# Six small constants placed first in SBUF, so that the 8 KB, 4 KB and 2 KB buffers begin at multiples of 1 KB

## The chip, the core and the metric

One core of a Trainium2 chip. Its engines are TensorE (PE in the profile; its weight loads are listed apart as PEld), VectorE (DVE), ScalarE (ACT), GpSimd (POOL) and SyncE (SP, which here only issues DMAs). Operands lie in SBUF, 128 partitions with an address within the partition; matmul results go to PSUM. The metric is the device time of one launch in microseconds, as the median of several runs.

## The reference

Two transformer blocks over one sequence of 512 tokens with 1024 features, all in float32. Cut to its shape:

```python
# first block
h = rms_norm(x, norm_g);  proj = h @ w_in
o_diff = diff_attention(...)                 # 4 heads, two softmaxes each
o_nsa  = g0 * compressed + g1 * selected + g2 * window     # 8 heads, 2 key heads
x = x + concat([o_diff * silu(dz), o_nsa * silu(nz)]) @ w_out
# second block
h = rms_norm(x, g_mix);  proj = h @ w_in_2
mixed = sigmoid gates over (short conv @ w_branch_a) and (top-256 attention @ w_branch_b)
x = x + mixed @ w_out_2
h = rms_norm(x, g_ffn)
x = x + (silu(h @ w_ffn_gate) * (h @ w_ffn_up)) @ w_ffn_down      # 1024 -> 2816 -> 1024
out = rms_norm(x, g_final)
```

## The kernel before

**Every large product is three matmuls.** A float32 operand is split into a rounded part (hi, written by ScalarE, lines 206 and 1272) and a remainder (lo, a subtraction on VectorE or GpSimd, lines 208 and 1273). `mm3` (line 171 on) then issues hi·hi, hi·lo and lo·hi into one PSUM bank, each a matmul of line 164 with its own load of the stationary operand: the load of the next matmul runs beside the matmul before it.

**Which operand stands still and which streams.** `gen_ii` (activations stand still, 256 to 320 weight columns stream), `gen_tt` (activations stand still, 512 weight columns stream), `gen_i` (weights stand still, 512 activation columns stream), and in the feed-forward `Pair.product` (line 1330): weights stand still, 256 columns of `hA` stream, 24 matmuls in a row. Between two products the feed-forward runs 12 matmuls of the down projection (`dn`, a `gen_ii`: activations `act` stand still, 256 weight columns stream).

**Where buffers lie.** A buffer belongs to a class (a tag of the pool), and a class is laid out when it is first asked for, in the order of the program text. Ahead of all classes lie 4,096 bytes of scratch and four constants of the framework, 32 bytes each, so the first class begins at 4,224, that is 128 past a multiple of 1,024. Before, the order was: `kf` (3 buffers of 4 KB), `k4` (13 of 4 KB), `k2` (19 of 2 KB), then `mhalf` (32 bytes), `identF` (512), the small class `sm` (28 of 96), `identR` (512), `ones` (32), then `k8` (13 of 8 KB), then the rest. So:

| class | what lies in it | start before | past a multiple of 1 KB |
|---|---|---|---|
| kf, k4 | raw weights, their hi and lo parts (`raw`, `whi`, `wlo`, `wh`, `wl`), attention probabilities `PTa` | 4,224 | 128 |
| k2 | 2 KB work tiles, weights of the down projection, `PTb` | 69,760 | 128 |
| k8 | activations as matmul operands: `hT`, `hA`, `act`, `qk`, `dV`, `yc`, `at`, `mg`, `oTd`, `oTn` | 112,448 | 832 |

Within a class every buffer has the same remainder, since their sizes are multiples of 1 KB. The parts of a buffer that matmuls read start a multiple of 512 bytes further on, except in the products with 264, 280 and 320 streamed columns. A pair of streamed and stationary operand from two different classes (k8 with k4 or k2) therefore starts 192 or 704 bytes apart, counted within 1 KB; a pair from one class, or from k4 and k2, starts 0 or 512 apart. The weights of the first two products of pairs 0 and 2 of the feed-forward (`begin`, line 1294, with `early`) are the one case in which the split weights are put into `k8` buffers: there the same product of 24 matmuls runs with both operands in `k8`.

Of the kernel before, what the change touches and what calls it, by code (L numbers as in the profile page):

```python
# [15 lines left out]
P = 128  # L16
# [31 lines left out]
class Kernel:  # L48
# [26 lines left out]
    def t(self, cls, shape, dt=F32, name="w"):  # L75
        return self.pool.tile(shape, dt, name=name, tag=cls, bufs=BUFS[cls])
# [104 lines left out]
    def tick(self):  # L181
        c, self.cost = getattr(self, "cost", 0.0), 0.0
        if self.filling and not self.busy:
            self.credit -= c
        self.spend(c)
# [66 lines left out]
def build(tc, pool, psum, dram, h):  # L252
    nc = tc.nc
    K = Kernel(tc, pool, psum, dram, h)
# [16 lines left out]
    S, MAKE = Lazy(), {}  # L271
# [10 lines left out]
    def f32(ap):  # L282
        return ap.bitcast(F32)
# [108 lines left out]
    def new_hT():  # L392
        return [[t("k8", [P, 4, T], F32R, "hT") for _ in range(2)] for _ in range(2)]
# [26 lines left out]
        return f  # L420


    xin = [t("kf" if tt < 3 else "k4", [P, D], F32, "xt") for tt in range(NT)]
    gB1 = t("k4", [P, D], F32, "gB")

    def x_load(tt):
        for c in range(XP):
            a = slice(c * D // XP, (c + 1) * D // XP)
            S["x"] = tc.keep_in_program_order(nc.sync.dma_start(xin[tt][:, a], x[tt * P:(tt + 1) * P, a])).ins

    grow = t("k2", [P, P], F32, "grow")[0:8]
    nc.scalar.dma_start(grow, h["norm_g"][0].rearrange("(r c) -> r c", c=P))
    x_load(0)

    mhalf = K.const([P, 1], "mhalf")
    V.memset(mhalf, -0.5)
    identF = K.const([P, P], "identF")
    make_identity(nc, identF)
    warm = ps([P, P], name="warm")
    for _ in range(WARM[0]):  # L440
# [13 lines left out]
        K.tr(warm, identF, identF)  # L454
    identR = K.const([P, P], "identR", F32R)
    G.tensor_copy(identR, identF)
    ones = K.const([P, 1], "ones")
    V.memset(ones, 1.0)


    S["hT"] = new_hT()

    NV = 65
    maskc = K.const([P, T], "maskc")
    DM = K.const([P, T], "DM")
    cmask = K.const([P, 4, 32], "cmask")
    rowok = K.const([P, 1], "rowok")
    qsc = K.const([P, 4, 2, 4], "qsc")
    cw2 = K.const([P, 2, 2, 64], "cw2")
    rbT = K.const([8, 32], "rbT")  # L470
# [2 lines left out]
    vec = K.const([P, NV], "vec")  # L473
    GD = K.const([P, 64], "GD")
    GN = K.const([P, 3, 64], "GN")
    c01 = K.const([P, 2], "c01")

    def constants():
        vrow = t("k2", [P, P], F32, "vrow")
# [336 lines left out]
        return evac  # L816


    KC = K.const([P, 64], "KC")

    def cmp_evac(m, o):
        v = m % 2
# [68 lines left out]
    def cmp_finish():  # L891
        for v in range(2):
# [5 lines left out]
            if v == 0:  # L898
# [12 lines left out]
                def go(kd=kd):  # L911
                    pk = ps([P, 64], name="pt")
                    K.tr(pk, kd[0:64].rearrange("p a d -> p (a d)"), identF[0:64, 0:64])
                    A.copy(KC, pk)
                    tick()
# [18 lines left out]
    def cmp_attention(g):  # L934
        st = {}

        def rows(tt):
            sc = ps([P, 4, 32], name="sc")
            for c in range(4):
                K.mm(sc[:, c, :], f32(S["nQ%d" % g][:, c, tt * P:(tt + 1) * P]), KC[:, g * 32:(g + 1) * 32],  # L940
                     c == 0, c == 3)
# [682 lines left out]
def emit(tc, h, stage="all"):  # L1624
    with tc.tile_pool(name="sb", bufs=1) as pool, \
            tc.tile_pool(name="ps", bufs=1, space=bass.MemoryType.PSUM) as psum, \
            tc.tile_pool(name="dr", bufs=1, space=bass.MemoryType.DRAM) as dram, \
            contextlib.nullcontext():
        build(tc, pool, psum, dram, h)
# [18 lines left out]
```

## Time and profile before

| | us |
|---|---|
| median of 3 runs | 1069.44 (1069.07 to 1070.16) |
| the profiled execution, its own time | 1070.19 |
| its span, first to last instruction | 1068.4 |
| TensorE busy in the span | 1043.4 (98%) |
| VectorE busy | 720.0 (67%) |
| ScalarE busy | 556.2 (52%) |
| GpSimd busy | 396.8 (37%) |
| DMA engines, queue 1, share of 16 | 32.6% |

The clock granted to TensorE is 0.994 over the whole span. Busy time of a matmul is modelled and overlaps with the next, so the rate of matmuls is read from starts, not from durations: the timeline merges equal neighbours into one row with its start and its count. In a triple hi·hi, hi·lo, lo·hi the first two have one name and the third another, so the starts of every second row are three matmuls apart.

### The profile page before, as it was taken

What the parts mean: (1) busy time and instruction counts of PE and PEld (TensorE: products, weight loads), DVE (VectorE), ACT (ScalarE), POOL (GpSimd) and SP (SyncE); (2) the same over time, 40 slices, a digit from 0 to 9 for tenths busy, and PEclk for the clock granted to TensorE, in tenths of its full rate; (3) what the DMA queues carried; (4) which work ended last, traced back from release to release, by engine and by line L of the source; (5) the groups of instructions that cost most, each with busy time, mean ns of one, the idle gap of its engine ahead of it and who ended that gap; (6) DMA issues with size and microseconds to landing.
All of it is one profiled execution on the core that took longest, in us unless ns stands there. A gap on an engine that the chain in (4) does not pass through costs nothing.

```text
span 1068.4 us, 18973 instructions
## 1 busy us (share of the span) xinstructions
PE 1043.4 (98%) x7257; PEld 962.7 (90%) x7257; DVE 720.0 (67%) x1468; ACT 556.2 (52%) x1155; POOL 396.8 (37%) x403
## 2 busy tenths in 40 slices
PE   6999999999999999999999999999999999999997
PEld 6999898899779899888888888989999999999995
DVE  5787467446994646999423653979987777777724
ACT  5476678647884445632323776436544444444433
POOL 3442357466367322112115875920012112121241
PEclk8999999999999999999999999999999999999999
DMA  5344421221114435335322323641433323333122
GB/s 167 114 138 136 102 62 41 58 82 60 57 43 129 140 92 167 100 98 155 112 79 69 90 70 108 237 139 60 158 109 119 117 82 100 94 114 109 31 90 79
DMA packets 128085, 109.69 MB, mean 103 GB/s; under 512 B 20393, under 2 KB 119154, under 8 KB 127994
## 3 DMA queue, kind: packets, MB, share of 16 engines
q1 hardware_dynamic: 126906, 105.83, 32.6%
q0 software_dynamic: 1072, 2.65, 0.7%
q8 instruction: 57, 0.93, 0.4%
q14 instruction: 34, 0.28, 0.1%
q10 hardware_dynamic: 16, 0.00, 0.0%
HBM read 103.13 MB, written 6.84 MB: 103 GB/s over the span
## 4 chain that ended last, share of the span: by engine, by line
PE 90%; DVE 4%; POOL 2%; ACT 2%; issue 1%; DMA 0%; SPq 0%; POOLq 0%; DVEq 0%; ACTq 0%
PE acc L164 76%; PE pt L178 5%; PE sc L164 4%; PE o L164 4%; POOL wlo L208 1%; ACT p L636 1%; DVE p L634 1%; DVE acc L1513 0%; POOL mg L1213 0%; DVE mg L1216 0%; PE warm L178 0%; DMA gv<-in_diff_k_norm_g 0%; ACT junk L380 0%; DVE PTa L653 0%; ACT whi L206 0%
## 5 line engine op out<-in xcount | busy, mean ns | idle before, releaser
L208 POOL TENSOR_TENSOR wlo<-raw,whi 128x1024 fp32r<-128x1024 f32 (+4 forms) x99 | 205.0, 2075 | 444.4 <-ACT whi L206 365.5
L164 PE MATMUL acc<-hA,wh 128*128 128x256 f32 x1264 | 218.0, 279 | 0.7 <-ACT wh L1272 0.7
L206 ACT CAST whi<-raw 128x1024 fp32r<-128x1024 f32 (+4 forms) x143 | 132.0, 924 | 125.1 <-PE acc L164 80.1
L164 PE MATMUL acc<-hT,whi 128*128 128x512 f32 x608 | 194.5, 398 | 0.0
L164 PEld LDWEIGHTS acc<-hA,wh 128*128 128x128 f32 x1264 | 189.0, 189 | 1.3 <-ACT wh L1272 0.9
L164 PE MATMUL acc<-whi,hT 128*128 128x256 f32 (+3 forms) x896 | 180.7, 290 | 1.0 <-DVE hT L402 1.0
L164 PE MATMUL acc<-hA,wl 128*128 128x256 f32 x584 | 162.4, 278 | 0.0
L164 PEld LDWEIGHTS acc<-whi,hT 128*128 128x128 f32 x896 | 144.1, 189 | 1.7 <-DVE hT L402 1.2
L164 PEld LDWEIGHTS acc<-hT,whi 128*128 128x128 f32 x608 | 112.2, 188 | 24.5 <-ACT r L1512 0.2
L164 PE MATMUL acc<-whi,act 128*128 128x256 f32 (+1 forms) x640 | 130.0, 289 | 0.0
L164 PE MATMUL acc<-wlo,hT 128*128 128x256 f32 (+3 forms) x448 | 128.6, 288 | 0.0
L164 PE MATMUL acc<-hT,wlo 128*128 128x512 f32 x304 | 120.9, 398 | 0.0
L164 PEld LDWEIGHTS acc<-hA,wl 128*128 128x128 f32 x584 | 109.6, 188 | 0.0
L164 PEld LDWEIGHTS acc<-whi,act 128*128 128x128 f32 x640 | 103.9, 188 | 2.5
L164 PE MATMUL acc<-wlo,act 128*128 128x256 f32 (+1 forms) x320 | 92.3, 289 | 0.0
L636 ACT ACTIVATE p<-p,s 128x128 f32<-128x128 f32 (+3 forms) x128 | 72.2, 565 | 29.9 <-DVE s L634 27.1
L164 PEld LDWEIGHTS acc<-wlo,hT 128*128 128x128 f32 x448 | 84.4, 189 | 0.4
L1272 ACT CAST wh<-raw 128x1024 fp32r<-128x1024 f32 x55 | 57.6, 1052 | 50.1 <-PE acc L164 43.6
L1273 DVE TENSOR_TENSOR wl<-raw,wh 128x1024 fp32r<-128x1024 f32 x51 | 63.3, 1245 | 29.8 <-PE acc L164 17.3
L208 DVE TENSOR_TENSOR wlo<-raw,whi 128x1024 fp32r<-128x1024 f32 (+5 forms) x44 | 53.6, 1221 | 42.3 <-ACT whi L206 42.2
L164 PEld LDWEIGHTS acc<-hT,wlo 128*128 128x128 f32 x304 | 57.2, 188 | 13.1
L164 PEld LDWEIGHTS acc<-wlo,act 128*128 128x128 f32 x320 | 60.1, 188 | 1.3
(279 smaller groups left out, 2044.4 us busy)
## 6 DMA issues: line engine op xcount, KB each, us to landing
raw<-in_w_in SPq DMA_DIRECT2D x52, 512.0 KB, 3.6
raw<-in_w_ffn_gate SPq DMA_DIRECT2D x28, 512.0 KB, 3.6
raw<-in_w_ffn_up SPq DMA_DIRECT2D x22, 512.0 KB, 4.6
raw<-in_w_ffn_down SPq DMA_DIRECT2D x36, 256.0 KB, 5.2
raw<-in_w_out SPq DMA_DIRECT2D x16, 512.0 KB, 3.3
raw<-in_cmp_w SPq DMA_DIRECT2D x8, 512.0 KB, 3.6
raw<-in_w_in SPq DMA_DIRECT2D x10, 384.0 KB, 3.4
rel_all<-rel_rows POOLq DMA_DIRECT2D x1, 2560.0 KB, 18.0
```

The lines of the kernel that those rows point to most:

```text
L164: self.nc.tensor.matmul(out, lhsT, rhs, start=start, stop=stop, skip_group_check=True)
L178: self.nc.tensor.transpose(out, in_, ident)
L206: self.nc.scalar.copy(hi, raw)
L208: (self.nc.gpsimd if every and self.split and self.split % every == 0 else self.nc.vector).tensor_tensor(lo, raw, hi.bitcast(F32), op=OP.s ...
L634: V.tensor_tensor_reduce(out=p[:, :n], in0=sc[:, :n], in1=bias, scale=-scale, scalar=3e38, op0=OP.add, op1=OP.min, accum_out=nm)
L636: S["exp"] = A.activation(p[:, :n], p[:, :n], AF.Exp, scale=-1.0, bias=nm, accum_out=z).ins
L1272: A.copy(hi, src)
L1273: eng.tensor_tensor(lo, src, f32(hi), op=OP.subtract)
```

## The change

Six constants that were asked for at different places are asked for first: `identF` (512 bytes), `KC` (256), `mhalf`, `ones`, `rowok` and `c01` (32 each), together 896 bytes. 4,224 + 896 = 5,120, a multiple of 1,024. And the first `k8` buffer is asked for right after the first `k2` buffer, ahead of `sm` and `identR`. In the built program all three big classes now start at a multiple of 1 KB (kf 5,120, k2 70,656, k8 109,568), and every pair of matmul operands from them starts 0 or 512 bytes apart within 1 KB, in the products with 264, 280 and 320 columns 0 or 256 or other multiples of 32.

Nothing else differs. On each of the five engines the instructions stand in the same order, with the same shapes, the same waits and the same semaphore values; only addresses, buffer numbers in names and line numbers differ. The order in the program text moved only where buffers are named: no instruction is added, removed or moved.

```diff
+    identF, KC = K.const([P, P], "identF"), K.const([P, 64], "KC")
+    mhalf, ones, rowok = [K.const([P, 1], name) for name in ("mhalf", "ones", "rowok")]
+    c01 = K.const([P, 2], "c01")
     xin = [t("kf" if tt < 3 else "k4", [P, D], F32, "xt") for tt in range(NT)]
     gB1 = t("k4", [P, D], F32, "gB")
...
     x_load(0)
-
-    mhalf = K.const([P, 1], "mhalf")
+    S["hT"] = new_hT()
+
     V.memset(mhalf, -0.5)
-    identF = K.const([P, P], "identF")
     make_identity(nc, identF)
...
-    ones = K.const([P, 1], "ones")
     V.memset(ones, 1.0)
-
-
-    S["hT"] = new_hT()
...
-    rowok = K.const([P, 1], "rowok")
...
-    c01 = K.const([P, 2], "c01")
...
-    KC = K.const([P, 64], "KC")
```

## Rows read from the trace of the kernel before

**Rows 1.** The page: busy times, and the chain that ended last by engine.
```profile
PE 1043.4 (98%) x7257; PEld 962.7 (90%) x7257; DVE 720.0 (67%) x1468; ACT 556.2 (52%) x1155; POOL 396.8 (37%) x403
...
PE 90%; DVE 4%; POOL 2%; ACT 2%; issue 1%; DMA 0%; SPq 0%; POOLq 0%; DVEq 0%; ACTq 0%
```

**Rows 2.** Windows: length, busy us (count) by engine, clock, DMA share, GB/s.
```profile
260.00:335.00 75.00, 70.23 (x510) 62.44 (x509) 60.83 (x234) 57.90 (x176) 39.82 (x47) 1.00 0.20 64
...
445.00:575.00 130.00, 130.00 (x559) 104.76 (x559) 82.09 (x150) 38.92 (x47) 24.26 (x13) 1.00 0.38 109
...
763.00:1061.00 298.00, 297.70 (x2472) 293.42 (x2472) 209.14 (x218) 127.43 (x182) 60.97 (x44) 1.00 0.30 96
```

**Rows 3.** Groups of matmuls with shapes: columns streamed, count, busy, mean ns.
```profile
L164 PE MATMUL acc<-hA,wh 128*128 128x256 f32 x1264 | 218.0, 279 | 0.7 <-ACT wh L1272 0.7
L164 PE MATMUL acc<-hT,whi 128*128 128x512 f32 x608 | 194.5, 398 | 0.0
L164 PE MATMUL acc<-hA,wl 128*128 128x256 f32 x584 | 162.4, 278 | 0.0
...
L164 PE MATMUL acc<-whi,hT 128*128 128x256 f32 x576 | 111.0, 284 | 1.0 <-DVE hT L402 1.0
L164 PE MATMUL acc<-whi,act 128*128 128x256 f32 x576 | 110.3, 278 | 0.0
...
L164 PE MATMUL acc<-wlo,act 128*128 128x256 f32 x288 | 79.9, 278 | 0.0
...
L164 PE MATMUL acc<-wlo,At 128*128 128x256 f32 x32 | 7.8, 279 | 0.0
```

**Rows 4.** Timeline of PE (start, length, count): products with both operands in k8.
```profile
717.46 5.92 PE L164 MATMUL acc<-hA,wh 128*128 128x256 f32 x48
...
725.32 6.00 PE L164 MATMUL acc<-hA,wh 128*128 128x256 f32 x48
```

**Rows 5.** Timeline of PE: products with hA in k8, weights in k4.
```profile
741.39 0.39 PE L164 MATMUL acc<-hA,wh 128*128 128x256 f32 x2
...
744.79 0.39 PE L164 MATMUL acc<-hA,wh 128*128 128x256 f32 x2
...
805.75 0.40 PE L164 MATMUL acc<-hA,wh 128*128 128x256 f32 x2
...
807.87 0.40 PE L164 MATMUL acc<-hA,wh 128*128 128x256 f32 x2
```

**Rows 6.** Timeline of PE: weights stream from k4 or k2, activations stand in k8.
```profile
215.38 0.40 PE L164 MATMUL acc<-whi,hT 128*128 128x256 f32 x2
...
221.03 0.40 PE L164 MATMUL acc<-whi,hT 128*128 128x256 f32 x2
...
804.26 0.39 PE L164 MATMUL acc<-whi,act 128*128 128x256 f32 x2
...
804.94 0.39 PE L164 MATMUL acc<-whi,act 128*128 128x256 f32 x2
```

**Rows 7.** Timeline of PE: 512 and 320 weight columns stream, activations stand in k8.
```profile
348.00 0.62 PE L164 MATMUL acc<-whi,oTn 128*128 128x512 f32 x2
...
350.06 0.62 PE L164 MATMUL acc<-whi,oTn 128*128 128x512 f32 x2
...
376.35 0.46 PE L164 MATMUL acc<-whi,hT 128*128 128x320 f32 x2
...
378.11 0.46 PE L164 MATMUL acc<-whi,hT 128*128 128x320 f32 x2
```

**Rows 8.** Timeline of PE: attention outputs with both operands in k4 or k2.
```profile
178.37 0.98 PE L164 MATMUL o<-PTa,nV 128*128 128x512 f32 x4
179.18 0.58 PE L164 MATMUL o<-PTb,nV 128*128 128x256 f32 x4
...
599.13 0.98 PE L164 MATMUL o<-PTa,bV 128*128 128x512 f32 x4
599.94 0.57 PE L164 MATMUL o<-PTb,bV 128*128 128x256 f32 x4
```

## The prediction, made before the changed kernel ran

> **What bounds the kernel now.** I read the page first. TensorE is busy 98% of the span and holds 90% of the chain that ended last; DMA has 0% of that chain and VectorE 4% [rows 1]. Then the windows: from 763 to 1061 us, the feed-forward, TensorE is busy 297.70 of 298.00 us, and from 445 to 575 us all of 130.00; the loosest stretch, 260 to 335 us, still has 70.23 of 75.00 [rows 2]. So a matmul that starts later by a nanosecond ends the kernel later by nearly a nanosecond, and what VectorE, ScalarE, GpSimd or the DMAs gain or lose is covered by TensorE as long as they stay as far from the bound as 67%, 52%, 37% and 32.6%.
>
> The change adds and removes no instruction. The one thing it can act on is how fast an operand comes out of SBUF, so the question is: does the rate of TensorE depend on where its two operands lie? For that I left the durations (a modelled end; 279 ns for 256 columns whatever the rate) and took differences of starts in the timeline, which is at full clock in all the stretches used.
>
> **The rate of one shape at different addresses.** All numbers are for 128 rows and 256 streamed columns unless said otherwise.
>
> - Streamed `hA` in k8, weights in k4 (192 or 704 bytes apart within 1 KB). From 741.39 to 744.79 us there are ten triples, thirty matmuls, in 3.40 us: 113.3 ns each. From 805.75 to 807.87 us six triples take 2.12 us: 117.8 ns [rows 5]. Both have the same class of addresses. In the steady part of the feed-forward whole products take turns at these two levels, mean 115.6 ns.
> - The same product with both operands in k8 (0 or 512 bytes apart). 48 matmuls in 5.92 us; less the last one's 0.28 us that is 5.64 us for 47 starts, 120.0 ns each. The other 48 take 6.00 us, 121.7 ns with one late start in it [rows 4]. All four products of this kind stand at 120; none of those in rows 5's place does.
> - Weights streamed from k4 or k2, activations standing in k8. From 215.38 to 221.03 us sixteen triples in 5.65 us: 117.7 ns; in the down projection at 804.26 to 804.94 us two triples in 0.68 us: 113.3 ns [rows 6]. The down projection keeps the level of the product ahead of it, so 115.6 ns on average; with 864 of 2176 matmuls there, the mean of this kind is (864 x 115.6 + 1312 x 117.7) / 2176 = 116.9 ns.
> - 512 columns: weights streamed, nine matmuls in 2.06 us, 228.9 ns [rows 7]; activations streamed from k8, 559 in 130.00 us, about 233 ns [rows 2]. 320 columns: twelve in 1.76 us, 146.7 ns [rows 7].
> - Both operands in k4 or k2 (again 0 or 512 apart): two of 512 and two of 384 columns take 0.81 us, twice [rows 8]. 1792 columns at the rate of 228.9 per 512 would be 0.80, at 233 per 512 0.82, at 120.0 per 256 0.84. So here a pair from one class costs nothing that four matmuls in a row can show.
>
> So the rate does go with the place: 1792 columns aside, a long run of a pair from one class is slower by 4.4 ns per matmul than the mean of the same shape from two classes. After the change every pair is what a pair from one class is now: 0 or 512 bytes apart.
>
> **The change part by part.** *Products of the feed-forward.* hA,wh 1264 and hA,wl 584, less the 96 whose weights are in k8 already: 1752 [rows 3]. They are exactly the instructions of rows 4, at the same relative places. 1752 x (120.0 - 115.6) = +7.7 us, all of it on the path, since that stretch has 0.3 us of slack.
>
> *Streamed weights, 256 columns.* Ten groups from x576 to x32, 2176 in all [rows 3]. No long run of this kind from one class is in the trace. Bounds: 0 by rows 8; 2176 x (120.0 - 116.9) = +6.7 us by rows 4. The roles of the operands lie between the two, so I take the half, +3.4.
>
> *512 columns.* 288 with streamed weights, from 228.9 ns: 0 to 288 x 4.1 = +1.2 us if they come to the 233 of the others; half, +0.6. The 1104 with streamed activations run at 233 already; rows 8 allow them 229 to 233, so 0 to -4.5 us; I take 0, because a pair from two classes and a pair from one cannot be told apart there.
>
> *320 columns.* 288 matmuls: 0 by rows 8 to 288 x (150.0 - 146.7) = +1.0 us at rows 4's rate per column; half, +0.5.
>
> *Everything else.* The split instructions read and write k4 next to k4, as before, so their operands lie to each other as before. DMAs now land at multiples of 1 KB; should they be quicker, the chain holds no share of them [rows 1], so nothing. `identF`, `ones`, `KC` move, with a few hundred transposes; no row prices that, and I take 0 with a bound of 1 us to either side.
>
> *Sum.* 7.7 + 3.4 + 0.6 + 0.5 = +12.2 us. Outside the feed-forward a part is covered where TensorE waits anyway (4.77 of 75 us in 260 to 335); of the 4.5 us outside products I let 1.2 be covered: **+11 us**. On the profiled execution 1070.19 + 11 = 1081.2; that execution is 0.75 us above the median, so on the median 1069.44 + 11 = **1080.4 us**, 1.0% slower. Its own range: from products that merely all stay at 117.8, 1752 x 2.2 = +3.9, to all upper ends, 7.7 + 6.7 + 1.2 + 1.0 = +16.6, so 1073.3 to 1086.
>
> **The rivals.** *Same.* The two levels of rows 5 come with addresses of one class, so something else than the place switches them, and the 120 of rows 4 could belong to that too (the high and low parts of those weights lie in one buffer). Rows 8 speak for it, the clean split (four products of four against none) against it. Then nothing moves: 1069.4, within 1067.3 to 1071.6.
>
> The Trainium skill (SBUF — State Buffer, "Who interferes with whom") would have this rival: it gives TensorE two independent read ports and says that it never waits on another engine, so a weight load takes nothing from a streaming matmul wherever the two lie. By that rule the sum is 0; the three rates of one shape in this trace show that it isn't the whole story.
>
> *Faster.* Not the distance between two operands counts but where each begins: now none begins at a multiple of 256 bytes (128 and 832 past 1 KB), and two operands that both begin 64 past a multiple of 128, as in rows 4, would be the worst case. After the change every one begins on a 256-byte boundary (the 264- and 280-column products aside), and all 256-column matmuls could run at 113.3, which rows 5 and 6 show to be possible: 1752 x 2.3 + 2176 x 3.6 = -11.8 us, 1057.6; with half of it 1063.5. It decides as soon as products average under 115.6 ns. Against it: in rows 8 both operands begin at a multiple of 128, better than the pairs of rows 5 by that reading, and they gain nothing.
>
> *The change doesn't do what it says.* The addresses were read from the built program; the three classes do begin at multiples of 1 KB, and the order of instructions is the same on each engine. I give it no chance.
>
> **How the numbers follow.** Slower as forecast 0.52; same 0.24; faster 0.24. A measurement of this kernel tells about 0.2%, 2.1 us, from no change; the ends of the forecast's own range lie beyond that, so these are the three chances too. The likeliest is the forecast: 1080.4. For 8 in 10: leaving out above 1086 costs about 0.03, and the faster case splits at about the middle between its half and its full effect, so with a lower end at 1061 another 0.12 is left out. Range 1061 to 1086, wide because the cases have both signs; of the likeliest alone it is 1073 to 1086.
>
> **What would show it.** In the changed kernel's timeline: products of the feed-forward at 120.0 ns per start, all of them, no longer taking turns (first term); the down projection and the projections of 256 streamed columns between 117 and 120 (second); 512-column stretches at 233 (third); the window of 298 us for the same 2472 matmuls longer by about 9 us; order and counts unchanged. Wrong if products still take turns at 113 and 118 (same), or stand at 113 or below throughout (faster); then the 120 of rows 4 is not a matter of the distance between operands within 1 KB.

## The result, and the profile after

| | median us | range | ratio to before |
|---|---|---|---|
| before, in the same comparison | 1069.39 | | |
| after | 1079.04 | 1077.51 to 1079.88 | 1.0090, 95% interval 1.0077 to 1.0103 |

The change costs 9.65 us, 0.9%; 11 were forecast. The two profiled executions are 1070.19 and 1079.68 us, +9.5, and the account below is between these two.

The page of the changed kernel, busy times and the chain by engine, against [rows 1]:

```profile
PE 1053.7 (98%) x7257; PEld 979.0 (91%) x7257; DVE 719.4 (67%) x1468; ACT 556.3 (52%) x1155; POOL 395.8 (37%) x403
...
PE 91%; DVE 5%; ACT 2%; DMA 1%; POOL 1%; issue 1%; POOLq 0%; DVEq 0%; ACTq 0%; SPq 0%
```

Same counts on every engine, VectorE, ScalarE and GpSimd within 1 us of what they were; TensorE alone is busy 10.3 us longer. The time is inside its matmuls. Which ones, the timeline says (start, length, count; the difference of two starts gives the rate). First the feed-forward product, against [rows 5], then 256 streamed weight columns, against [rows 6], and 512 of them, against [rows 7]:

```profile
806.86 0.40 PE L164 MATMUL acc<-hA,wh 128*128 128x256 f32 x2
...
808.66 0.40 PE L164 MATMUL acc<-hA,wh 128*128 128x256 f32 x2
...
215.75 0.40 PE L164 MATMUL acc<-whi,hT 128*128 128x256 f32 x2
...
221.51 0.40 PE L164 MATMUL acc<-whi,hT 128*128 128x256 f32 x2
...
349.50 0.62 PE L164 MATMUL acc<-whi,oTn 128*128 128x512 f32 x2
...
351.54 0.62 PE L164 MATMUL acc<-whi,oTn 128*128 128x512 f32 x2
```

Five triples in 1.80 us are 120.0 ns per matmul, sixteen in 5.76 us are 120.0 (117.7 before), and three triples of 512 columns in 2.04 us are 226.7 (228.9 before). So 256 columns became slower and 512 columns **faster**. The second is larger where the activations stream. Eight triples of hT by whi and wlo in the kernel before, and seven in the changed one:

```profile
470.14 0.63 PE L164 MATMUL acc<-hT,whi 128*128 128x512 f32 x2
...
475.74 0.63 PE L164 MATMUL acc<-hT,whi 128*128 128x512 f32 x2
```

```profile
470.50 0.61 PE L164 MATMUL acc<-hT,whi 128*128 128x512 f32 x2
...
475.26 0.61 PE L164 MATMUL acc<-hT,whi 128*128 128x512 f32 x2
```

5.60 us for 24 starts are 233.3 ns, 4.76 us for 21 are 226.7.

Setting each matmul of the changed trace beside the same one before gives the lag of the changed kernel along the program. It is +1.3 us at 430, jumps by 3.1 to +4.4 at 450, **falls** to -0.5 by 710 (the 512-column projections lie there), and climbs in the feed-forward by about 0.7 us in every 20 to +9.7 at 1050. The jump is a wait that the kernel before does not have. Windows of the changed kernel around it (length, busy us and count by engine, granted clock, DMA share, GB/s), then PE's waits from 440 to 450 us:

```profile
440.00:447.00 7.00, 5.61 (x30) 4.38 (x28) 7.00 (x15) 5.79 (x17) 2.38 (x1) 1.00 0.26 71
447.00:450.00 3.00, 2.91 (x13) 2.56 (x14) 3.00 (x10) 1.93 (x4) 0.00 (x0) 0.59 0.05 13
450.00:455.00 5.00, 5.00 (x21) 4.05 (x21) 3.71 (x9) 0.13 (x1) 0.00 (x0) 0.90 0.31 84
```

```profile
PE pt L178 <- DVE bV L1166: 1.5, 1, 1.5
```

TensorE waits 1.48 us for VectorE ahead of a group of transposes, and right after that the clock is granted at 0.59 for 3 us and 0.90 for 5, so part of that time at the lower of its two levels (1.2 GHz). VectorE is busy all through both windows that surround the wait. What holds it up is one of its own instructions, an accumulation over 512 columns that starts beside a weight split (`wlo`) on GpSimd. VectorE, then GpSimd, in the kernel before and in the changed one:

```profile
442.58 0.75 DVE L1513 SCALAR_TENSOR_TENSOR acc<-r,iws,acc 128x512 f32<-128x512 f32 x1
...
444.03 2.11 DVE L1513 SCALAR_TENSOR_TENSOR acc<-r,iws,acc 128x512 f32<-128x512 f32 x1
...
442.67 2.92 POOL L208 TENSOR_TENSOR wlo<-raw,whi 128x1024 fp32r<-128x1024 f32 x1 [10.73 <-DVE qs L1161]
```

```profile
443.94 2.87 DVE L1510 SCALAR_TENSOR_TENSOR acc<-r,iws,acc 128x512 f32<-128x512 f32 x1
...
443.88 2.38 POOL L208 TENSOR_TENSOR wlo<-raw,whi 128x1024 fp32r<-128x1024 f32 x1 [10.60 <-PE acc L164]
```

Before, the accumulation starts 0.09 us ahead of the split and takes 0.75 us; a later one, behind the `bV` that the transposes need, takes 2.11. In the changed kernel the split starts first, and the same accumulation takes 2.87 us and ends 0.55 us after the split does; `bV` and the transposes come behind it. So the wait is a matter of which of the two is first.

### The profile page after: what moved, and what is told of

Read it like the earlier page. It is cut to its first block, busy times and chain, and to the rows that moved or that the text cites. A ratio compares the mean times of both kernels' runs of the same rounds, so it can differ in the third digit from the quotient of the medians.

```text
span 1077.9 us, 18973 instructions
## 1 busy us (share of the span) xinstructions
PE 1053.7 (98%) x7257; PEld 979.0 (91%) x7257; DVE 719.4 (67%) x1468; ACT 556.3 (52%) x1155; POOL 395.8 (37%) x403
## 4 chain that ended last, share of the span: by engine, by line
PE 91%; DVE 5%; ACT 2%; DMA 1%; POOL 1%; issue 1%; POOLq 0%; DVEq 0%; ACTq 0%; SPq 0%
PE acc L164 78%; PE pt L178 5%; PE sc L164 4%; PE o L164 4%; ACT p L634 1%; DMA raw<-in_w_ffn_up 1%; DVE p L632 1%; DVE acc L1510 0%; DVE mg L1213 0%; PE warm L178 0%; DMA raw<-in_w_out 0%; DVE hA L1398 0%; DVE PTa L651 0%; ACT PTa L650 0%; POOL p L1020 0%
## 5 line engine op out<-in xcount | busy, mean ns | idle before, releaser
L164 PE MATMUL acc<-hA,wh 128*128 128x256 f32 x1264 | 225.4, 283 | 0.2 <-ACT wh L1269 0.2
L164 PEld LDWEIGHTS acc<-hA,wh 128*128 128x128 f32 x1264 | 193.9, 192 | 0.8 <-ACT wh L1269 0.4
L164 PE MATMUL acc<-hT,whi 128*128 128x512 f32 x608 | 192.3, 395 | 0.0
L164 PE MATMUL acc<-whi,hT 128*128 128x256 f32 (+3 forms) x896 | 183.2, 293 | 0.0
L164 PE MATMUL acc<-hA,wl 128*128 128x256 f32 x584 | 165.1, 283 | 0.0
L164 PEld LDWEIGHTS acc<-whi,hT 128*128 128x128 f32 x896 | 146.3, 191 | 0.5
L164 PE MATMUL acc<-whi,act 128*128 128x256 f32 (+1 forms) x640 | 133.4, 294 | 0.0
L164 PEld LDWEIGHTS acc<-hA,wl 128*128 128x128 f32 x584 | 112.0, 192 | 0.0
L164 PEld LDWEIGHTS acc<-whi,act 128*128 128x128 f32 x640 | 106.3, 192 | 2.5
```

Source lines behind the costliest of these rows:

```text
L164: self.nc.tensor.matmul(out, lhsT, rhs, start=start, stop=stop, skip_group_check=True)
```

## The experiments

**The rate by itself.** What the whole kernel shows mixed was measured with nothing else running, in one execution. `mov` and `sta` are two SBUF buffers that begin at a multiple of 1 KB; each group is

```python
for dm, ds in PAIRS if turn == 0 else PAIRS[::-1]:
    o = psum.tile([P, 512], F32, name="n%dm%ds%dx" % (n, dm, ds), tag="ps", bufs=8)
    for j in range(8):
        k, f = j % 4, j // 4
        a = [sta[:, ds // 4 + 1024 * l + 256 * k + 128 * f:][:, 0:P] for l in range(2)]
        b = [mov[:, dm // 4 + 2048 * l + n * k:][:, 0:n] for l in range(2)]
        for x, y in ((a[0], b[0]), (a[0], b[1]), (a[1], b[0])):
            nc.tensor.matmul(o[:, 0:n], x, y, start=j == 0, stop=j == 7, skip_group_check=True)
```

(`dm` and `ds` are bytes past a multiple of 1 KB.)

> This run leaves the whole computation out and only multiplies: groups of 24 matmuls of the kernel's own pattern (three products of split halves for each of eight slices), the streamed operand and the stationary operand each put at a chosen offset within 1 KB of SBUF, 20 pairs of offsets, 256 and 512 columns, in two turns with the second reversed. Theory A (what counts is the distance of the two operands within 1 KB): the pairs at distance 0, that is (0, 0), (64, 64), (128, 128) and (832, 832), all take 120.0 ns at 256 columns and about 227 at 512; (832, 128) and (704, 0) read alike, at 113 to 118 ns for 256 and 229 to 233 for 512. Theory B (what counts is that each operand begins at a multiple of 1 KB): (0, 0) stands apart from (64, 64), (128, 128) and (832, 832) by 3 ns or more, and (704, 0) is not as (832, 128). Theory C (the operands' places count for nothing, the change moved the time by another way): all 20 pairs agree within 1 ns at each size.

Its timeline, in the second turn (`n256m832s128x`: 256 columns, streamed operand at 832, stationary at 128):

```profile
186.60 2.99 PE L78 MATMUL n256m832s128x<-mov,sta 128*128 128x256 f32 x24
189.43 3.04 PE L78 MATMUL n256m832s832x<-mov,sta 128*128 128x256 f32 x24
192.31 3.03 PE L78 MATMUL n256m128s128x<-mov,sta 128*128 128x256 f32 x24
195.18 3.02 PE L78 MATMUL n256m64s64x<-mov,sta 128*128 128x256 f32 x24
...
203.73 2.88 PE L78 MATMUL n256m0s192x<-mov,sta 128*128 128x256 f32 x24
206.45 3.00 PE L78 MATMUL n256m0s128x<-mov,sta 128*128 128x256 f32 x24
...
245.79 5.76 PE L78 MATMUL n512m832s128x<-mov,sta 128*128 128x512 f32 x24
251.38 5.63 PE L78 MATMUL n512m832s832x<-mov,sta 128*128 128x512 f32 x24
...
278.76 5.66 PE L78 MATMUL n512m0s192x<-mov,sta 128*128 128x512 f32 x24
284.26 5.75 PE L78 MATMUL n512m0s128x<-mov,sta 128*128 128x512 f32 x24
...
295.45 5.75 PE L78 MATMUL n512m704s0x<-mov,sta 128*128 128x512 f32 x24
301.04 5.76 PE L78 MATMUL n512m448s0x<-mov,sta 128*128 128x512 f32 x24
```

The start of the next group less that of a group, divided by 24, is its rate: (832, 832) takes 2.88 us, 120.0 ns; (0, 192) takes 2.72, 113.3 by these rounded starts; (832, 128) of 512 columns 5.59, 232.9; (832, 832) of 512 columns 5.48, 228.3 (the group after it begins at 256.86). Both turns together, by starts to the nanosecond, without the very first group, which starts slowly:

| streamed minus stationary, within 256 bytes | pairs | 256 columns, ns | 512 columns, ns |
|---|---|---|---|
| 0 | 0/0, 64/64, 128/128, 832/832, 256/0, 0/256 | 119.0 to 120.1 | 227.1 to 228.8 |
| 32 | 32/0 | 117.1 to 118.0 | 233.5 |
| 64 | 64/0, 0/192, 0/704, 128/832 | 113.5 to 118.0 | 228.9 to 229.8 |
| 96 | 96/0 | 119.4 to 119.8 | 233.8 |
| 128 | 128/0, 0/128, 384/0 | 118.2 to 118.9 | 232.0 to 233.3 |
| 192 | 192/0, 448/0, 704/0, 0/64, 832/128 | 113.5 to 117.9 | 233.0 to 233.3 |

Theory A holds in a narrower form than expected: the distance counts within 256 bytes, not 1 KB. Theory B falls: 64/64 and 128/128 are as slow as 0/0. Theory C falls. And 256 and 512 columns order the distances differently: 0 is the worst for the one, with 96 close to it, and the best for the other. At 64 and 192 a 256-column group has two rates, about 113.4 and 117.8, and one pair can show either (64/0 took 118.0 in one turn and 113.5 in the other).

**The parts of the change apart.** Only the 8 KB class early, so that all classes begin at 128 past a multiple of 1 KB (against the kernel before):

```diff
     x_load(0)
+    S["hT"] = new_hT()
...
-    S["hT"] = new_hT()
```

> The constants stay where they were and only the 8 KB buffers are placed before them, so that all three classes begin at 128 above a multiple of 1 KB: distance 0 as in the changed kernel, and no class on a multiple of 1 KB. Theory A (distance): as the changed kernel, 1077 to 1081 us, with the 256-column products of the feed-forward part at 120.0 ns and its 512-column ones at 227. Theory B (absolute start): as the kernel before, 1067 to 1072 us, or a third value. Theory C (something else than the places of the matmuls' operands, such as the places of the small constants): 1067 to 1072 us, since the constants lie where they lay.

It took 1077.78 us, ratio 1.0074 (1.0055 to 1.0092). Its products and its 512 columns:

```profile
808.18 0.40 PE L164 MATMUL acc<-hA,wh 128*128 128x256 f32 x2
...
810.70 0.40 PE L164 MATMUL acc<-hA,wh 128*128 128x256 f32 x2
...
470.10 0.62 PE L164 MATMUL acc<-hT,whi 128*128 128x512 f32 x2
...
475.54 0.62 PE L164 MATMUL acc<-hT,whi 128*128 128x512 f32 x2
```

Seven triples in 2.52 us, 120.0 ns, and eight of 512 columns in 5.44 us, 226.7: the changed kernel's rates with nothing on a multiple of 1 KB. The alignment that the change is about plays no part.

The opposite: 896 bytes of small constants first (with `qsc` in place of four of the six) and 4 KB and 2 KB aligned as in the changed kernel, but 8 KB at 704. Against the changed kernel, in part:

```diff
-    mhalf, ones, rowok = [K.const([P, 1], name) for name in ("mhalf", "ones", "rowok")]
-    c01 = K.const([P, 2], "c01")
+    qsc = K.const([P, 4, 2, 4], "qsc")
...
+    mhalf, ones = K.const([P, 1], "mhalf"), K.const([P, 1], "ones")
+    sm(1)
     S["hT"] = new_hT()
```

> The 4 KB and 2 KB classes begin at a multiple of 1 KB as in the changed kernel, the 8 KB class at 704 above one: the distance between the classes is that of the kernel before. Theory A (distance): as the kernel before, 1067 to 1072 us, hA by the up weights at 116 ns of 256 columns and hT by whi at 233 of 512. Theory B (absolute start): the weights are aligned and the 8 KB buffers are not, so at least 1073 us, with the products whose two operands lie in the 4 KB class as in the changed kernel. Theory C (the places of the small constants, placed first here too): as the changed kernel, 1077 to 1081 us.

1068.38 us, ratio 0.9988 (0.9977 to 0.9998): the kernel before, within 0.2%. Theories B and C fall once more.

Constants first and the 8 KB class late, at a distance of 128; against the changed kernel:

```diff
     x_load(0)
-    S["hT"] = new_hT()
...
+    S["hT"] = new_hT()
 
     NV = 65
```

> The constants alone are placed first and the 8 KB buffers stay late: the 4 KB and 2 KB classes begin at a multiple of 1 KB, the 8 KB class at 128 above one, a distance of 128 that neither kernel had. Theory A (distance): a third value of its own, for the 256- and 512-column forms across the two classes alone, as the groups at (128, 0) and (0, 128) of the run with multiplications only give it; the forms with both operands in one class stay at 120.0 ns. By the two distances known it would lie between 1066 and 1081 us. Theory B (absolute start): between the two kernels, 1070 to 1079 us. Theory C (small constants): as the changed kernel, 1077 to 1081 us.

1079.23 us, 1.0089 (1.0070 to 1.0107), inside the wide band of theory A, though theory C's figure would fit it too. What tells them apart is the products:

```profile
808.39 0.40 PE L164 MATMUL acc<-hA,wh 128*128 128x256 f32 x2
...
810.88 0.40 PE L164 MATMUL acc<-hA,wh 128*128 128x256 f32 x2
```

Seven triples in 2.49 us are 118.6 ns, the rate of distance 128 in the table and neither kernel's. With 233 for 512 columns it loses less on the one side and gains nothing on the other.

**A distance that beats both.** If the table is right, 8 KB at 64 above 4 KB instead of 192 keeps the 256-column rates, brings streamed activations of 512 columns from 233 to 229.5 and takes streamed weights of 512 columns from 229 to 233.

```diff
     mhalf = K.const([P, 1], "mhalf")
+    ones = K.const([P, 1], "ones")
+    S["hT"] = new_hT()
```

(and both taken from where they stood). 

> Two 32-byte constants and the 8 KB class are placed before the other constants: the 4 KB and 2 KB classes stay at 128 above a multiple of 1 KB and the 8 KB class comes to 64 above them, where it was 704, or 192 within 256 bytes, above them. Theory A, narrowed by the run with multiplications only (what counts is the distance of the two operands within 256 bytes, streamed minus stationary: 256 columns take 113 to 118 ns at 64 and at 192 and 120 at 0; 512 columns take 227 at 0, 229.5 at 64, 233.2 at 192): the forms with streamed activations of 512 columns (hT, yc, at with whi and wlo, 1061 matmuls) fall from 233.3 to 229.5 ns, -4.0 us; those with streamed weights (281) rise from 229 to 233, +1.1 us; the 256-column forms stay at 113 to 118. Together 1066.5 us, 1064.5 to 1068.5. Rival (the distance within 1 KB counts, or 64 and 704 differ otherwise): 1069 us or more, since 64 within 1 KB would be a distance of its own.

1065.93 us (1064.44 to 1067.45), ratio 0.9971 (0.9959 to 0.9983): faster than both kernels, by 3.2 us against before where 2.9 were expected. Its hT products:

```profile
469.67 0.62 PE L164 MATMUL acc<-hT,whi 128*128 128x512 f32 x2
...
475.17 0.62 PE L164 MATMUL acc<-hT,whi 128*128 128x512 f32 x2
```

Eight triples in 5.50 us, 229.2 ns. By back-to-back starts in the profiled execution, streamed activations of 512 columns give -4.1 us and streamed weights +1.2, as expected (-4.0 and +1.1). Two terms nobody expected are in the total as well, the same 1.5 us wait (+1.6) and more of the 256-column projections at the fast one of their two rates (-1.9); that they cancel is luck (the rest makes +0.3).

**The two rates of 256 columns.** In the kernel before, 31 of the 64 stretches of hA products between down projections run at 113 to 114 ns (start-to-start means) and the others at 118; the rate changes where act gives way to hA, a step from distance 64 to 192. In `swap`, with the two distances exchanged, it changes where hA gives way to act, again from 64 to 192, and again 31 of 64 are fast. So I moved the 2 KB class as well, by a 128-byte constant (`qsc`) between the 4 KB and the 2 KB class, to give both forms one distance. `same64`, and `same192` without the line of `rbT`:

```diff
     gB1 = t("k4", [P, D], F32, "gB")
+    qsc = K.const([P, 4, 2, 4], "qsc")
...
     mhalf = K.const([P, 1], "mhalf")
+    ones = K.const([P, 1], "ones")
+    rbT = K.const([8, 32], "rbT")
+    S["hT"] = new_hT()
```

> As the run named swap, with the 2 KB class moved too, so that hA by wh and wl (8 KB against 4 KB) and the streamed down weights by act (2 KB against 8 KB) both stand at 64 within 256 bytes, where the kernel before has them at 192 and at 64. In the kernel before the feed-forward products run either at 113.4 or at 117.8 ns, and change from one to the other where act gives way to hA. Theory A1 (the change between these two rates comes from the step between the distances 64 and 192): with one distance there is no change, and the feed-forward part runs at one of the rates throughout, so about 1060 us if that is 113.4 (2600 matmuls by -2.3 ns on top of swap's -3), or 1072 us if it is 117.8. Theory A2 (the change has another source, such as the count of matmuls in a group): the two rates still take turns, 1064.5 to 1068.5 us as swap.

> The 8 KB class at 192 above the 4 KB class within 256 bytes as in the kernel before, and the 2 KB class moved so that both feed-forward forms stand at 192. The 512-column forms stay at 233 (streamed activations) and 229 (streamed weights). Theory A1: the feed-forward part runs at one rate throughout, 1063 us at 113.4 or 1075 us at 117.8. Theory A2: the two rates take turns as before, 1067 to 1072 us.

`same64` took 1071.08 us, 1.0019 (1.0010 to 1.0028), `same192` 1071.62 us, 1.0024 (1.0014 to 1.0034). Two stretches of hA and the down projection between them, in `same64` and then in `same192`:

```profile
806.24 0.40 PE L164 MATMUL acc<-hA,wh 128*128 128x256 f32 x2
...
808.71 0.40 PE L164 MATMUL acc<-hA,wh 128*128 128x256 f32 x2
...
809.30 0.40 PE L164 MATMUL acc<-whi,act 128*128 128x256 f32 x2
...
810.72 0.40 PE L164 MATMUL acc<-whi,act 128*128 128x256 f32 x2
```

```profile
807.90 0.39 PE L164 MATMUL acc<-whi,act 128*128 128x256 f32 x2
...
808.25 0.39 PE L164 MATMUL acc<-whi,act 128*128 128x256 f32 x2
...
808.59 0.39 PE L164 MATMUL acc<-whi,act 128*128 128x256 f32 x2
...
808.93 0.28 PE L164 MATMUL acc<-whi,act 128*128 128x256 f32 x1
...
809.04 0.40 PE L164 MATMUL acc<-hA,wh 128*128 128x256 f32 x2
...
811.51 0.40 PE L164 MATMUL acc<-hA,wh 128*128 128x256 f32 x2
```

In `same64` hA stands at 117.6 ns (2.47 us for 21) and act at 118.3 (1.42 us for 12), from the first stretch to the last: no turns, at the slow rate, the upper of the two times expected. In `same192` hA stands at 117.6 (2.47 us for 21) and act at 115.0 on the mean: after a few slower starts it runs at 113.3 (0.68 us for 6). These are turns, though other ones, with no step of distance at all. So A1's expectation came true for distance 64 and not for 192, where the time lies in the range of A2.

Could the fast rate be entered from other absolute places? Three shifts of `same64`, by 64, 128 and 192 bytes of constants placed first; the last of them:

```diff
+    iws = K.const([P, NT, 8], "iws")
+    rowok = K.const([P, 1], "rowok")
+    c01 = K.const([P, 2], "c01")
     xin = [t("kf" if tt < 3 else "k4", [P, D], F32, "xt") for tt in range(NT)]
```

> The kernel of the run same64 with two 32-byte constants first, so that every class lies 64 bytes higher and all distances stay. In same64 the feed-forward products ran at 117.8 ns from the first to the last, without taking turns. Theory A3 (which of the two rates is entered follows from the absolute places, and then stays, since one distance gives no change): the rate may come out as 113.4 here, then 1060 to 1063 us; otherwise 1069 to 1073 us; nothing between, because no turns are taken. Rival (the rate is a matter of the moment at which the stalled products start again, not of the places): 1069 to 1073 us in all three shifts, or different rates in different executions of one kernel.

> As same64, every class 128 bytes higher. Theory A3: 1060 to 1063 us or 1069 to 1073 us, nothing between. Rival: 1069 to 1073 us as same64.

> As same64, every class 192 bytes higher. Theory A3: 1060 to 1063 us or 1069 to 1073 us, nothing between. Rival: 1069 to 1073 us as same64.

1071.41, 1070.79 and 1070.78 us, each 1.0016 to 1.0022 times before, and all stretches at 118. In these three A3's chance of a fast entry didn't come; no shift of the absolute places changed anything.

Last, a step from 64 to 192 put in by hand, and its control with the operands exchanged:

```diff
             a = S["hA" + {...}[n]]
+            if self.d == 3 and n == "1":
+                for _ in range(6):
+                    nc.tensor.matmul(bank[:, 0, :], a[:, 0, 0, 0:P], wh[:, 0, :], start=True, stop=True, skip_group_check=True)
```

> The kernel of the run same64 with six matmuls of 256 columns put ahead of the first product of the fourth block of the feed-forward part; their result is overwritten. They stream a weight (4 KB class) past a stationary hA (8 KB class), a distance of 192 within 256 bytes, between products that all stand at 64. Theory A1 (the step from 64 to 192 changes the rate, the step back does not): from there on the products run at 113.4 ns where they ran at 117.8. Eight of eleven blocks follow, about 1340 matmuls of hA and 780 of act, by -4.4 ns = -9.3 us, and the six cost 0.7: 1062.5 us, 1061 to 1065, with the feed-forward stretch free of turns. Rival (the rate doesn't change by a few matmuls at another distance, but by what the whole neighbouring group is): 1071 to 1073 us.

> The same six matmuls at the same place with their two operands exchanged: hA streamed past the weight, the distance of 64 that the neighbours have. Both theories: no change of rate, 1071 to 1073 us. If it falls to 1062 us too, an interruption of the groups changes the rate and not the distance, and theory A1 falls.

1071.60 us for the step and 1071.85 for the control. Around the six in the run with the step:

```profile
780.97 0.87 PE L1335 MATMUL acc<-wh,hA 128*128 128x256 f32 x6
781.67 0.40 PE L164 MATMUL acc<-hA,wh 128*128 128x256 f32 x2
...
783.79 0.40 PE L164 MATMUL acc<-hA,wh 128*128 128x256 f32 x2
```

0.70 us for six and 2.12 us for the next eighteen: 116.7 and 117.8 ns. Six matmuls at 192 change nothing, so the step of distance by itself is not what switches the rate, and with the turns of `same192` A1 falls as a mechanism. (All six read one and the same pair of operands, which no group of the kernel does.)

Up to the six, at 780.97 us, `flip` is `same64`: the same addresses and the same order. Yet its first long stretch of products runs at the other rate. First `flip`, then `same64`:

```profile
740.20 0.39 PE L164 MATMUL acc<-hA,wh 128*128 128x256 f32 x2
...
743.60 0.39 PE L164 MATMUL acc<-hA,wh 128*128 128x256 f32 x2
```

```profile
740.03 0.40 PE L164 MATMUL acc<-hA,wh 128*128 128x256 f32 x2
...
743.56 0.40 PE L164 MATMUL acc<-hA,wh 128*128 128x256 f32 x2
```

Ten triples in 3.40 us, 113.3 ns, against 3.53 us, 117.7 ns. From 764 us on `flip` is slow as well. So addresses and order of instructions together do not fix the rate: one layout showed both, which the rival in the expectation of `same64_at64` allows for (different rates in different executions). That the moment at which products start again decides, as that rival has it, is not shown. What does switch the rate **stays open**.

## Why the prediction came out as it did

The sign and the cause were right: the distance between the operands, not the start of each, is what the change acts on, and the products came to 120.0. The terms, with start-to-start means over all back-to-back matmuls of a form in the two traces ("found" counts those starts):

| term of the sum | forecast | measured |
|---|---|---|
| products hA by wh and wl | +7.7 | 116.0 and 115.4 to 120.0, 1841 found: **+7.7** |
| streamed weights, 256 columns | +3.4, from 0 to +6.7 | act +3.6, hT +1.9, oTd, mg and At +1.1: **+6.6** |
| streamed weights, 512 columns | +0.6 | 229 to 227.2, 281 found: **-0.5** |
| streamed activations, 512 columns | 0, from 0 to -4.5 | hT -4.7, yc -0.6, at -0.6: **-5.9** |
| 320 columns | +0.5 | 146.7 to 146.7: **0** |
| covered by waits | -1.2 | the new wait and its clock: **+3.1** |

- **Products.** Right in mechanism and size. The 96 matmuls of [rows 4] were the same instructions at the distance that all got, and that was enough.
- **256 streamed columns with weights on the move.** Mis-sized: half was taken between two bounds, and the upper bound was the value. The reason given, that the roles of the operands lie between [rows 4] and [rows 8], doesn't hold: the runs show one rate at distance 0 in either role. Long runs at 120 were the better guide than the short groups of [rows 8].
- **512 columns.** Here the step failed. [rows 8] were read as a pair from one class that gains nothing, since two of 512 and two of 384 columns in 0.81 us agreed with the rates of [rows 7]. They agree as well with 227 and 176 ns, (2 x 227 + 2 x 176) = 806 ns: four matmuls, timed to 10 ns, cannot tell 227 from 229, and the prediction said so, but took 0 for the streamed activations and a loss for the streamed weights. The bound of -4.5 was too near as well, since it stopped at 229 and 227 was to be had. The inference that one distance is slow for every width was the wrong one.
- **Waits.** The forecast let slack swallow 1.2 us. In this execution a wait appeared instead, in the one region where the products had become faster. With the lower clock behind it, it gave back half of what the 512 columns earned; VectorE's 67% on the average, by which the prediction took it for covered, says nothing of such a moment. `k8_early`, `swap`, `same64`, `same64_at64` and `flip_control` have the same 1.5 us wait; the kernel before, `consts_first`, `k8_704` and `same192`, without faster 512 columns, don't have it; nor do `same64_at128`, `same64_at192` and `flip`, with faster ones. The order of GpSimd's split and VectorE's accumulation fits all thirteen traces: with the wait the split starts first by 16 to 58 ns, without it by at most 9 ns, or later. And this order goes with the rate of the 512 columns: at 233 ns the split starts 69 to 88 ns behind the accumulation, at about 229 it starts 0 to 30 ns ahead, so near a tie that it falls either way, and at 227 it starts 53 and 58 ahead. That the wait comes of this collision is shown; that the faster columns bring it on is read from these thirteen, and no run moves the split alone.
- **The sum.** The measured column makes +11.0, +7.9 of it rates, and the executions differ by 9.5. The 870 other starts that do not follow back to back stand 1.65 us closer in all, which makes up for the 1.5 us; why they do is open. The total came near because errors met: +3.2 too little for 256 columns, 7.0 too much for 512, and a wait of 3 that was not forecast.
- **The rivals.** "Same" fell: the two levels of [rows 5] do switch without a change of address, as it said (`flip` and `same64`), but the 120 of [rows 4] is a third level and belongs to the distance. "Faster" by absolute starts fell with `k8_early` and with 64/64, which was to be the worst case and read like 0/0. Of the four signs named for the changed kernel three came: products at 120.0 without turns, streamed 256 columns at 119.2 to 120.0, and a feed-forward about 10 us longer by the lag, where 9 were named; 512 columns did not stay at 233.

The run with multiplications only leaves every other engine idle and still spreads one shape over 113.5 to 120.1 ns. The Trainium skill (SBUF — State Buffer, "Who interferes with whom") gives TensorE two independent read ports that share with no engine; these runs do not contradict that other engines leave it alone, but they do not agree with reading it as a rate that is free of where the two operands lie.

## What to carry to other kernels

In these traces a float32r matmul's rate depends on where its two operands begin relative to each other, so before a layout is changed, list for each shape which classes its operands come from and take the distance within 256 bytes; "aligned" means distance 0, which was the best for 512 columns and the worst for 256. Rates that differ by 2 to 6% are read from differences of starts over a long run, never from the durations of single matmuls nor from groups of four. Where TensorE fills the span, such a layout is worth trying by itself: the 8 KB class at 64 instead of 704 bytes past the 4 KB class gave 0.3%.

## What was not expected of the hardware

- One shape at several distances: 256 columns at 113.3 to 120.1 ns, 512 columns at 226.7 to 233.8, with distance 0 the slowest for the one and the fastest for the other, and a period of 256 bytes (256/0 and 0/256 read like 0/0).
- Two rates at one distance, 113.4 and 117.8 ns, that hold for hundreds of matmuls and change at places the program repeats. What changes them is open: a step of distance of six matmuls doesn't, and one layout with one order of instructions showed both (`flip` and `same64`).
- After a wait of 1.48 us TensorE's granted clock stood at 0.59 for the next 3 us and cost about as much again as the wait. In `k8_early` the same wait was followed by a clock of 1.00, so it isn't the wait alone.
- VectorE's accumulation of 128x512 took 0.73 to 0.75 us where it started before GpSimd's 128x1024 split or at most 9 ns behind its start, and 2.87 to 2.92 where it started 16 to 58 ns behind, in all six such traces with its end 0.55 us after the split's. An order that turns on less than 0.1 us cost TensorE 1.5.
